# Picking and placing tokens for 32 experts: fp32 one-hot products with transposes become float32r products with two-part operands, on 16 weight slots

## The chip, the cores and the metric

The kernel runs on one core of a Trainium2 chip. The metric is device time in microseconds of one execution, as the median of several runs. Engines are named as in the profile: PE is TensorE's matmul stream, PEld its weight loads, DVE is VectorE, ACT is ScalarE, POOL is GpSimd, SP is SyncE, whose queue issues the loads of the weights.

## The reference, cut to what matters

Two layers of a hybrid block, then a layer with attention and a linear recurrence, and then the part that the change is in, a mixture of 32 experts over 256 tokens of 1024 features. Everything is float32.

```python
def moe_ffn(xn, w_router, b_router, w_gate, b_gate, w_up, b_up, w_down, b_down):
    logits = (xf @ w_router + b_router).astype(jnp.float32)      # xf: 256 x 1024
    top_v, top_i = lax.top_k(logits, TOP_K)                      # 4 of 32 experts
    gates = jax.nn.softmax(top_v, axis=-1).astype(xn.dtype)
    ...                                        # tokens sorted by expert
    def expert_block(args):
        xb, e = args
        g = xb @ w_gate[e] + b_gate[e]         # 1024 x 1024 each
        u = xb @ w_up[e] + b_up[e]
        g = jnp.minimum(g, SWIGLU_LIMIT)
        u = jnp.clip(u, -SWIGLU_LIMIT, SWIGLU_LIMIT)
        glu = g * jax.nn.sigmoid(SWIGLU_ALPHA * g)
        return ((u + 1.0) * glu) @ w_down[e] + b_down[e]
    ...                                        # times the gate, summed into the tokens
```

The layer adds the result to x, and a last rms norm follows.

## The kernel before, in words

Up to about 480 us the first three layers run. Their weights come through the same slots as the experts'. A slot is a tile of 128 x 2048 floats (1 MB) in SBUF; there are 24, and `give` (L235) hands free ones to the list `order` of all weight tiles, in order: for every tile of the list it issues one DMA on the SP queue (L243). `release` (L247) gives a slot back when its tile has been used. For the experts, slots 0 to 3, 8, 9, 13, 15 to 18 and 21 are given first (L1016, L1017), then 4 to 7 and 11 (L1033), then 10 and 14 (L1298): 19 in all. An expert has 12 tiles, four each of gate, up and down.

`router` (L1095) computes the logits, the four gates and, for each token and expert, `rank`, the token's place among that expert's tokens (1000 or more for tokens of other experts), and `count`. It also makes `xh`, the normed x (L1114).

The loop over the experts handles 64 tokens (CAP) of each:

- `pick` (L1178) compares rank with the numbers 0 to 63 (`hot`, 128 tokens x 64 places, for both halves of the tokens), multiplies `hot` transposed with `xh` in fp32 (L1186, PSUM bank xg), copies (L1187), transposes four blocks (L1192) and multiplies them with the norm's gain into `xT` (L1194). `pick` of the next expert is written behind the gating of this one.
- `up` (L1227) multiplies xT with the gate's and the up part's tiles (`product`, L1214, banks g and u; the two halves of 512 columns go to two 64-column halves of the array), with the bias as one float32r product of a one-hot `own` (L1230, L1234).
- `gated` (L1240) is five passes: clamp of g (L1242), tanh on ACT (L1243), a product (L1244), clamp of u (L1245), and the product that gives h (L1246).
- `place` (L1198), at odd experts for two of them: one-hots times gates (`hotw`, L1205), four transposes (L1210, bank st), a copy into `back` (L1212).
- `add`, through `add_pair`, at even experts for the two before: per half of the tokens two fp32 products of `back` with the experts' outputs `ys` (L1266, two buffers of bank cb) and two adds into x on DVE (L1269), each 512 columns.
- The branch `If` at L1278 (`more_up`) runs the same again for an expert with more than 64 tokens. Then gate's and up's eight slots are released. `down` (L1248) transposes h (L1251), copies (L1253) and multiplies with the down tiles (bank y); two copies, one on ACT (L1326) and one on DVE (L1328), give `ys`. The branch at L1284 (`more_down`) handles further tokens, and the four slots of down are released.

The order on each engine is set by a scheduler that takes the instructions by their place in the program as they become ready; an `If` with its body is one unit to it, and instructions outside may be moved past it. So a pick or an add may stand ahead of the branch at L1278 or behind it. In this run two experts have more than 64 tokens: their second passes stand in the trace at about 545 to 590 us and 1440 to 1480 us.

Of the kernel before, what the change touches and what calls it, by code (L numbers as in the profile page):

```python
# [17 lines left out]
CAP = 64  # L18
# [8 lines left out]
def _col_layout():  # L27
    at, off = {}, 0
    for name, n in (
        ("norm0", 8), ("norm1", 8), ("y0", 4), ("y1", 4), ("cw0", 16), ("cw1", 16), ("cb0", 4), ("cb1", 4),  # L30
        ("n1g", 8), ("final", 8), ("cw2", 16), ("cb2", 4), ("ba", 8), ("bi", 8), ("lam", 8), ("og", 8), ("n2g", 8),
    ):
        at[name] = (off, n)
        off += n
    return at, off
# [62 lines left out]
def _prep(i):  # L98
# [52 lines left out]
    put("n2g", a["norm2_g_2"][0])  # L151
    z["cols"] = c
# [43 lines left out]
def _build(tc, T, out):  # L196
# [577 lines left out]
    def mixer(xt):  # L774
# [258 lines left out]
        give(4, 5, 6, 7, 11)  # L1033
# [41 lines left out]
    t22, t23 = slot(22), slot(23)  # L1075
    xh = slot(12).rearrange("p (a b) -> p a b", a=2)
    bias = ew.tile([128, 1024], F32R, name="bias")
    xg, th = t22[:, 0:512], t22[:, 512:1024]
    more_h = [t22[:, 1024:1536], t22[:, 1536:2048], ew.tile([128, 512], F32, name="more")]
    ys, xTs = ([t23[:, o + 512 * k:o + 512 * k + 512] for k in range(2)] for o in (0, 1024))  # L1080
    nc.scalar.dma_start(rbc[0:96, :], T["b_down"])
    gates, rank = (sm(n, 2, 32, bufs=1) for n in ("gates", "rank"))
    count = small.tile([1, 32], I32, name="count", bufs=1)

    t14 = slot(14)

    def split_bias():

        b = t14[:, 256:1280]
        nc.scalar.dma_start(b, T["bias"])  # L1090
        S.activation(bias, b, AF.Copy)
        for p in (slice(32, 64), slice(96, 128)):
            V.tensor_tensor(bias[p], b[p], bias[p].bitcast(F32), op=OP.subtract)

    def router():  # L1095
# [7 lines left out]
        r, _ = x_stats(1e-5, xh, False, True)  # L1103
        tt = [bank(n) for n in ("xg", "tr", "st", "y")]
# [8 lines left out]
        for hf in range(2):  # L1113
            V.tensor_scalar(xh[:, hf, :], x[:, hf, :], r[:, hf:hf + 1], None, op0=OP.mult)  # L1114
# [33 lines left out]
    def last_bias():  # L1148

        t = bank("tr")  # L1150
        gx = ew.tile([128, 2, 192], F32, name="hotw")[:, :, 0:96]
# [15 lines left out]
    four = lambda v: v.rearrange("p (c s t) -> p c s t", c=4, s=2)  # L1167
    gain = cols[:, COLS["n2g"][0]:COLS["n2g"][0] + 8].rearrange("p (s c) -> p c s", s=2)

    def ranks(e, j):  # L1170
        if not j:
            return rank[:, :, e]
        r = sm("rj", 2)
        V.tensor_scalar(r, rank[:, :, e], -64.0 * j, None, op0=OP.add)
        return r

    def pick(e, j):

        r = ranks(e, j)
        one_hot = ew.tile([128, 2, 64], F32, name="hot", bufs=2)  # L1180
# [188 lines left out]
```

## Time and profile before

| | us |
|---|---|
| median of 3 runs | 1564.4 |
| lowest and highest | 1557.71, 1566.32 |
| profiled execution, its own time | 1557.0 |
| span in the profile | 1555.1 |
| PE busy | 1406.8 (90%) |
| DVE busy | 580.6 (37%) |
| ACT busy | 306.7 (20%) |
| moved by DMA | 469.31 MB, mean 302 GB/s |

The page cuts the span in 40 slices of 38.9 us. The timeline lists instructions by start, duration, engine, line, operation and tiles, merged where they follow each other; in brackets stands how long the engine was idle before and what ended that. An fp32 product stands as two records in PE's stream, a float32r product as one. A matmul's duration holds its way through the array, so the work that it costs in a row of them is the spacing of their starts. Tiles that lie in slots are all named s.

### The profile page before, as it was taken

The page shows a single profiled execution, that of the slowest core. Times are in us where ns is not written, and L with a number is a line of the kernel's source. Part 1 is how long each engine was busy: PE and PEld are TensorE (multiplying, and loading weights), DVE is VectorE, ACT ScalarE, POOL GpSimd, SP SyncE. Part 2 cuts the span into 40 slices and gives each one's busy share as a digit, 9 for nine tenths or more (in the row PEclk, how much of TensorE's full clock was granted, in tenths as well). Part 3 has the DMA queues.
Part 4 walks back from the last instruction along what each step waited for, and adds up shares of the span by engine and source line. Part 5 has one row for each costly group of instructions (what it writes and reads, how often), then busy time and mean ns, then how long its engine had stood idle before and what let it go on. Part 6 is the DMA issues. An engine that isn't in the chain of part 4 may idle for free. (4 is left out here: it accounts for less than half of the span.)

```text
span 1555.1 us, 17575 instructions
## 1 busy us (share of the span) xinstructions
PE 1406.8 (90%) x6638; PEld 707.5 (45%) x6638; DVE 580.6 (37%) x1238; ACT 306.7 (20%) x551; POOL 170.8 (11%) x100
## 2 busy tenths in 40 slices
PE   7899989999879989999899999998999998999896
PEld 6687877888556333333333333333333333333332
DVE  4856467648786212222122212221222222222123
ACT  4335443454552000000000000000000000000001
POOL 3333333344240000000000000000000000000001
PEclk9899999999889999999999999999999999999998
DMA  8423443444258756999999999999999999999561
GB/s 296 160 91 127 137 163 109 142 148 139 81 196 337 297 210 264 419 417 370 412 401 420 407 416 408 377 419 418 417 418 410 419 419 406 413 420 419 235 252 63
DMA packets 67500, 469.31 MB, mean 302 GB/s; under 512 B 8128, under 2 KB 9440, under 8 KB 11744
## 3 DMA queue, kind: packets, MB, share of 16 engines
q1 hardware_dynamic: 65664, 463.38, 74.4%
q8 instruction: 142, 2.33, 0.6%
q10 hardware_dynamic: 1632, 3.10, 0.6%
q14 instruction: 62, 0.51, 0.1%
HBM read 465.40 MB, written 1.05 MB: 300 GB/s over the span
## 5 line engine op out<-in xcount | busy, mean ns | idle before, releaser
L1223 PE MATMUL g<-s,s 128*64 128x512 f32 x1088 | 289.4, 601 | 25.3 <-PEq L1284 23.4
L1223 PE MATMUL y<-s,hT 128*64 128x512 f32 x1088 | 256.5, 602 | 1.8 <-ACT hT L1253 1.8
L1223 PE MATMUL u<-s,s 128*64 128x512 f32 x1088 | 247.5, 596 | 0.0
L1223 PEld LDWEIGHTS g<-s,s 128*64 128x64 f32 x1088 | 83.3, 136 | 179.1 <-issue 175.2
L1223 PEld LDWEIGHTS y<-s,hT 128*64 128x64 f32 x1088 | 91.5, 139 | 148.4 <-issue 124.7
L355 POOL TENSOR_TENSOR s<-s,s 128x1024 fp32r<-128x1024 f32 (+2 forms) x59 | 135.3, 2296 | 215.6 <-ACT s L352 163.5
L1223 PEld LDWEIGHTS u<-s,s 128*64 128x64 f32 x1088 | 74.6, 137 | 142.7 <-issue 139.3
L1328 DVE COPY s<-y 64x512 f32<-64x512 f32 x32 | 22.0, 689 | 297.4 <-ACTq L1284 280.6
L1343 POOL TENSOR_TENSOR s<-x,s 128x512 f32<-128x512 f32 x4 | 4.9, 1266 | 1081.2 <-DVE x L1269 1081.2
L352 ACT ACTIVATE s<-s 128x1024 fp32r<-128x1024 f32 (+2 forms) x100 | 100.0, 1008 | 115.9 <-PE pja L370 54.5
L369 PE MATMUL pjb<-s,s 128*128 128x512 f32 (+2 forms) x288 | 101.1, 351 | 7.6 <-DVE s L355 7.6
L368 PE MATMUL pjb<-s,s 128*128 128x512 f32 (+2 forms) x288 | 102.0, 354 | 1.1 <-ACT s L399 0.7
L368 PE MATMUL pja<-s,s 128*128 128x512 f32 (+2 forms) x272 | 98.8, 364 | 3.1 <-ACT s L352 2.6
L370 PE MATMUL pjb<-s,s 128*128 128x512 f32 (+2 forms) x288 | 100.3, 348 | 1.2 <-DVE s L355 0.8
L369 PE MATMUL pja<-s,s 128*128 128x512 f32 (+2 forms) x272 | 97.4, 358 | 3.6 <-DVE s L355 3.6
L370 PE MATMUL pja<-s,s 128*128 128x512 f32 (+2 forms) x272 | 96.7, 355 | 0.5 <-DVE s L400 0.5
L1245 DVE TENSOR_SCALAR s<-u 128x512 f32<-128x512 f32 x34 | 23.5, 692 | 178.2 <-PE u L1223 178.2
L355 DVE TENSOR_TENSOR s<-s,s 128x1024 fp32r<-128x1024 f32 (+2 forms) x53 | 69.4, 1312 | 52.7 <-ACT s L352 52.5
L1242 DVE TENSOR_SCALAR gm<-g 128x512 f32<-128x512 f32 x32 | 22.1, 692 | 161.4 <-PE g L1223 161.4
L1186 PE MATMUL xg<-s,hot 128*64 128x512 f32 x272 | 78.4, 599 | 2.5 <-DVE hot L1182 2.5
L1243 ACT ACTIVATE s<-gm 128x512 f32<-128x512 f32 x32 | 20.2, 630 | 303.2 <-DVE gm L1242 303.2
L1269 DVE TENSOR_TENSOR x<-x,cb 128x512 f32<-128x512 f32 x72 | 49.1, 687 | 64.9 <-PE cb L1266 64.8
(357 smaller groups left out, 1509.8 us busy)
## 6 DMA issues: line engine op xcount, KB each, us to landing
s<-in_w_up_dram SPq DMA_DIRECT2D x128, 1024.0 KB, 18.0
s<-in_w_gate_dram SPq DMA_DIRECT2D x128, 1024.0 KB, 18.1
s<-in_w_down_dram SPq DMA_DIRECT2D x128, 1024.0 KB, 12.3
s<-in_w_o_dram SPq DMA_DIRECT2D x12, 1024.0 KB, 4.8
s<-in_w_cqk_dram SPq DMA_DIRECT2D x4, 1024.0 KB, 7.9
s<-in_w_bqk_dram SPq DMA_DIRECT2D x4, 1024.0 KB, 4.9
s<-in_w_bvg_dram SPq DMA_DIRECT2D x4, 1024.0 KB, 5.0
s<-in_w_aq_dram SPq DMA_DIRECT2D x4, 1024.0 KB, 4.8
```

The lines of the kernel that those rows point to most:

```text
L352: S.activation(h, w, AF.Copy)
L355: (V if el == "V" else G).tensor_tensor(lo, w, h.bitcast(F32), op=OP.subtract)
L368: PE.matmul(d, ah, bh, start=start, stop=False, skip_group_check=True)
L369: PE.matmul(d, ah, bl, start=False, stop=False, skip_group_check=True)
L370: PE.matmul(d, al, bh, start=False, stop=stop, skip_group_check=True)
L1186: ins = PE.matmul(t[64 * c:64 * c + 64, :], one_hot[:, hf, :], xh[:, hf, 512 * c:512 * c + 512], start=hf == 0, stop=hf == 1)
L1223: ins = PE.matmul(t[o:o + 64, :], a[:, kt % 4, kt // 4, :], w[i][:, 1024 * k + 512 * c:1024 * k + 512 * c + 512], start=kt == 0, stop=kt == 7)
L1242: V.tensor_scalar(gm, tt[0], 7.0, None, op0=OP.min)
L1243: S.activation(th, gm, AF.Tanh, scale=0.851)
L1245: V.tensor_scalar(th, tt[1], 7.0, -7.0, op0=OP.min, op1=OP.max)
L1269: V.tensor_tensor(d, d, t[c], op=OP.add)
L1328: cp(ys[c][p, :], t[p, :])
```

## The change

- Slots: 11, 10 and 14 are no longer given to weights; 16 stay. The slots 12, 23, 22, 10, 11 and 14 hold the expert stage's own tiles.
- The normed x is kept as two float32r parts, `xp[0]` (rounded, on ACT) and `xp[1]` (the rest, on DVE).
- `pick(b, q)` makes the transposed inputs of four experts (batch b) at once: for two of the eight blocks of features, four float32r products each of an x block (128 x 128, the weights) with the one-hots of four experts (256 columns), and an ACT pass with the gain. It is called once per expert, a quarter of the next batch at a time; ahead of the loop four times for batch 0. The copies and transposes of the old pick are gone.
- `places(e)`, now for every expert: a one-hot of 128 x 128; one float32r product that spreads the expert's row of ranks over 128 partitions, two of two columns that pick the gates of the places; three small DVE passes, the last of which compares the spread ranks with the place numbers and gives `back`.
- `down` ends with two passes that scale y with the gates and split it in two float32r parts `yp` (ACT, then DVE).
- `scatter(hf)`, for every expert and one expert later: per half of the tokens four float32r products of 64 rows (two parts, two halves of 512 columns) and two adds into x.
- In `more_down` the scatters of the first 64 tokens and `places` come ahead of the second `down`; its own scatter is left to the next expert's.

```diff
-        give(4, 5, 6, 7, 11)
+        give(4, 5, 6, 7)
...
+    xp = [slot(i, F32R).rearrange("p (a b) -> p a b", a=2) for i in (12, 23)]
...
         for hf in range(2):
-            V.tensor_scalar(xh[:, hf, :], x[:, hf, :], r[:, hf:hf + 1], None, op0=OP.mult)
+            S.activation(xp[0][:, hf, :], x[:, hf, :], AF.Copy, scale=r[:, hf:hf + 1])
+            V.scalar_tensor_tensor(xp[1][:, hf, :], x[:, hf, :], r[:, hf:hf + 1], xp[0][:, hf, :].bitcast(F32),
+                                   op0=OP.mult, op1=OP.subtract)
...
+    xTs = [slot(i).rearrange("p (k n) -> p k n", k=8) for i in (22, 10)]
+    f11, f14 = slot(11), slot(14, F32R)
+    hid, th, hT, xTm = (f11[:, o:o + 512] for o in range(0, 2048, 512))
+    yp = [f14[:, o:o + 512] for o in (0, 512)]
+    hot = f14[:, 1024:1536].rearrange("p (a e s) -> p a e s", a=2, e=4)
+    back, hotm = f14[:, 1536:1792], f14[:, 1792:2048].rearrange("p (a s) -> p a s", a=2)
...
+    def one_hots(b):
+
+        for hf in range(2):
+            V.tensor_tensor(hot[:, hf], rank[:, hf, 4 * b:4 * b + 4, None].to_broadcast([128, 4, 64]),
+                            slots[:, None, 0:64].to_broadcast([128, 4, 64]), op=OP.is_equal)
...
+    def places(e, j):
+
+        one_hot(e, j)
         t = bank("st")
+        PE.matmul(t[:, 0:256], idr[:, e:e + 1].to_broadcast([32, 128]), rT, start=True, stop=True)
+        for hf in range(2):
+            PE.matmul(t[:, 256:258], hotm[:, hf, :], gp[:, hf, e, :], start=hf == 0, stop=hf == 1)
+        g, gs = sm("gj", 1), sm("gs", 2)
+        V.tensor_copy(gs, t[:, 256:258])
+        V.tensor_tensor(g, gs[:, 0:1], gs[:, 1:2], op=OP.add)
+        V.tensor_scalar(back, t[:, 0:256], -64.0 * j, col("slotp", 0), op0=OP.add, op1=OP.is_equal)
+        return g
+
+    def pick(b, q):
+
+        t = two(bank("pk"))
+        for i in range(2):
+            kt = 2 * q + i
             for hf in range(2):
+                for k in range(2):
+                    PE.matmul(t[:, i, :], xp[k][:, hf, 128 * kt:128 * kt + 128], hot[:, hf].rearrange("p e s -> p (e s)"),
+                              start=hf + k == 0, stop=hf + k == 2)
+        for i in range(2):
+            S.activation(xTs[b % 2][:, 2 * q + i, :], t[:, i, :], AF.Copy, scale=gain[:, 2 * q + i:2 * q + i + 1])
...
+    def pick_more(e, j):
+
+        one_hot(e, j)
+        t = bank("tr").rearrange("p (k n) -> p k n", k=8)
+        for kt in range(8):
+            for hf in range(2):
+                for k in range(2):
+                    PE.matmul(t[:, kt, :], xp[k][:, hf, 128 * kt:128 * kt + 128], hotm[:, hf, 0:64], start=hf + k == 0, stop=hf + k == 2)
+        V.tensor_tensor(xTm, t, gain[:, :, None].to_broadcast([128, 8, 64]), op=OP.mult)
+        return xTm
...
-    def add(lhs, rhs):
-        for hf in range(2):
-            t = [bank("cb", 2) for _ in range(2)]
+        S.activation(yp[0], t, AF.Copy, scale=g)
+        V.scalar_tensor_tensor(yp[1], t, g, yp[0].bitcast(F32), op0=OP.mult, op1=OP.subtract)
+
+    def scatter(hf):
+
+        t = [bank("cb", 2) for _ in range(2)]
+        for k in range(2):
             for c in range(2):
-                PE.matmul(t[c], lhs(c, hf), rhs(c), start=True, stop=True)
-            for c in range(2):
-                d = x[:, hf, 512 * c:512 * c + 512]
-                V.tensor_tensor(d, d, t[c], op=OP.add)
+                p = slice(64 * c, 64 * c + 64)
+                PE.matmul(t[c], back[p, 128 * hf:128 * hf + 128], yp[k][p, :], start=k == 0, stop=k == 1)
+        for c in range(2):
+            d = x[:, hf, 512 * c:512 * c + 512]
+            V.tensor_tensor(d, d, t[c], op=OP.add)
...
-        gated(t, h, h)
-        if e < 31:
-            cur = pick(e + 1, 0)
-        if e % 2:
-            back = place([(e - 1, 0), (e, 0)], "back")
-        elif e:
-            add_pair()
+        gated(t, hid, hid)
+        if e:
+            scatter(0)
+        if b < 7:
+            pick(b + 1, i)
+        if e:
+            scatter(1)
         if e == 6:
             last_bias()
+        g = places(e, 0)
         n = nc.values_load(count[0:1, e:e + 1], min_val=0, max_val=256)
         more_up(e, w, n, 1)
```

## Rows read from the trace of the kernel before

**Rows 1.** The page: the span, and DMA in 40 slices.
```profile
span 1555.1 us, 17575 instructions
...
DMA  8423443444258756999999999999999999999561
GB/s 296 160 91 127 137 163 109 142 148 139 81 196 337 297 210 264 419 417 370 412 401 420 407 416 408 377 419 418 417 418 410 419 419 406 413 420 419 235 252 63
```

**Rows 2.** Windows: stretch, length, busy PE, PEld, DVE, ACT, POOL, PEclk, DMA share, GB/s.
```profile
611.00:984.00 373.00, 345.42 (x1457) 121.37 (x1456) 87.76 (x178) 28.28 (x47) 0.00 (x0) 0.99 0.99 406
984.00:1410.00 426.00, 393.24 (x1685) 140.76 (x1685) 99.85 (x206) 33.82 (x56) 0.00 (x0) 1.00 1.00 413
```

**Rows 3.** Waits of the SP queue, 984 to 1410: us in total, times, longest.
```profile
SPq L243 <- PEq L1278: 179.2, 15, 18.2
```

**Rows 4.** Waits of PE, 984 to 1410.
```profile
PE g L1223 <- PEq L1284: 15.4, 14, 1.9
PE tr L1251 <- DVEq L1278: 14.6, 14, 1.1
```

**Rows 5.** Timeline, an even expert between u and y.
```profile
1160.85 1.89 PE L1186 MATMUL xg<-s,hot 128*64 128x512 f32 x8
1161.06 0.69 DVE L1245 TENSOR_SCALAR s<-u 128x512 f32<-128x512 f32 x1 [5.37 <-PE u L1223]
...
1162.66 1.13 PE L1266 MATMUL cb<-s,back 128*128 128x512 f32 x2
...
1163.63 0.60 PE L1192 MATMUL tr<-cst,s 128*128 128x128 f32 x4
...
1164.06 2.93 PE L1266 MATMUL cb<-s,back 128*128 128x512 f32 x6
...
1167.03 0.69 DVE L1269 TENSOR_TENSOR x<-x,cb 128x512 f32<-128x512 f32 x1 [0.36 <-PE cb L1266]
...
1168.12 0.63 PE L1251 MATMUL tr<-cst,gm 128*128 128x128 f32 x4 [1.13 <-DVEq L1278]
```

**Rows 6.** Timeline of DVE, the odd expert before it.
```profile
1131.35 0.69 DVE L1245 TENSOR_SCALAR s<-u 128x512 f32<-128x512 f32 x1 [5.37 <-PE u L1223]
...
1135.57 0.23 DVE L1230 TENSOR_SCALAR own<-cst 128x128 fp32r<-128x128 f32 x1 [0.40 <-DVEq L1278]
```

**Rows 7.** Groups by line and form, whole span: busy us, mean ns, idle before.
```profile
L355 DVE TENSOR_TENSOR s<-s,s 128x1024 fp32r<-128x1024 f32 x48 | 64.7, 1350 | 35.9 <-ACT s L352 35.8
...
L399 ACT ACTIVATE s<-tr,cols 128x256 fp32r<-128x256 f32 x20 | 9.4, 472 | 19.6 <-PE tr L407 15.8 <-DVE s L400 3.8
```

**Rows 8.** Timeline of PE, an expert of the stretch 611 to 984.
```profile
767.11 0.63 PE L1251 MATMUL tr<-cst,gm 128*128 128x128 f32 x4 [1.88 <-DVEq L1278]
...
771.97 1.45 PE L1186 MATMUL xg<-s,hot 128*64 128x512 f32 x5
...
779.82 1.88 PE L1266 MATMUL cb<-s,back 128*128 128x512 f32 x4
```

**Rows 9.** Timeline of PE, first layer: float32r products of 512 and of 256 columns.
```profile
200.47 0.39 PE L370 MATMUL pjb<-s,s 128*128 128x512 f32 x1
200.70 0.28 PE L368 MATMUL pja<-s,s 128*128 128x256 f32 x1
200.81 0.28 PE L369 MATMUL pja<-s,s 128*128 128x256 f32 x1
```

**Rows 10.** Timeline of PE, attention scores: fp32 products of 64 rows.
```profile
408.72 1.16 PE L898 MATMUL sc<-s 64*128 64x256 f32 x8
```

**Rows 11.** Timeline of PE: the start of u ahead of rows 5.
```profile
1153.39 5.32 PE L1223 MATMUL u<-s,s 128*64 128x512 f32 x24
```

**Rows 12.** Timeline of DVE, the normed x ahead of the router's passes.
```profile
486.23 1.41 DVE L1114 TENSOR_SCALAR s<-x,rr 128x1024 f32<-128x1024 f32 x2
```

**Rows 13.** Timeline of PE, from the first pick to the first g.
```profile
492.10 1.94 PE L1186 MATMUL xg<-s,hot 128*64 128x512 f32 x8
...
496.23 0.64 PE L1223 MATMUL g<-s,s 128*64 128x512 f32 x1
```

More of the change, by code (lines that the diff above doesn't have):

```diff
@@ L1074, in _build @@
     ew = ctx.enter_context(tc.tile_pool(name="ew", bufs=1))
-    t22, t23 = slot(22), slot(23)
-    xh = slot(12).rearrange("p (a b) -> p a b", a=2)
     bias = ew.tile([128, 1024], F32R, name="bias")
-    xg, th = t22[:, 0:512], t22[:, 512:1024]
-    more_h = [t22[:, 1024:1536], t22[:, 1536:2048], ew.tile([128, 512], F32, name="more")]
-    ys, xTs = ([t23[:, o + 512 * k:o + 512 * k + 512] for k in range(2)] for o in (0, 1024))
+    more_h = [ew.tile([128, 512], F32, name=f"more{j}") for j in range(3)]
     nc.scalar.dma_start(rbc[0:96, :], T["b_down"])
@@ L1102, in router @@
         load_row(br, "br")
-        r, _ = x_stats(1e-5, xh, False, True)
-        tt = [bank(n) for n in ("xg", "tr", "st", "y")]
+        r, _ = x_stats(1e-5, two(slot(22)), False, True)
+        tt = [bank(n) for n in ("pk", "tr", "st", "y")]
         x_T(0, [two(t) for t in tt])
@@ L1166, in _build @@
     nc.scalar.dma_start(b_down, T["b_down_end"])
[L1167 to L1180, printed above, removed]
-        for hf in range(2):
-            V.tensor_scalar(one_hot[:, hf, :], slots[:, 0:64], r[:, hf:hf + 1], None, op0=OP.is_equal)
-        t = bank("xg")
-        for hf in range(2):
-            for c in range(2):
-                ins = PE.matmul(t[64 * c:64 * c + 64, :], one_hot[:, hf, :], xh[:, hf, 512 * c:512 * c + 512], start=hf == 0, stop=hf == 1)
-        S.activation(xg, t, AF.Copy)
-        if e + j == 0:
-            busy(ins, 2, bank("cb", 2))
-        t = bank("tr")
-        for c in range(4):
-            PE.transpose(t[:, 128 * c:128 * c + 128], xg[:, 128 * c:128 * c + 128], ident)
-        xT = four(more_h[j - 1] if j else xTs[e % 2])
-        V.tensor_tensor(xT, four(t), gain[:, :, :, None].to_broadcast([128, 4, 2, 64]), op=OP.mult)
-        return xT
@@ L1284, in more_down @@
         with tc.If(n > CAP * j, label=f"down{e}_{j}"):
-            y = more_h[j - 1]
-            t = down(y, w)
-            busy(last[0], 4, bank("cb", 2))
-            S.activation(y, t, AF.Copy)
-            back = place([(e, j)], "backm")
-            half = lambda c: slice(64 * c, 64 * c + 64)
-            add(lambda c, hf: back[half(c), 128 * hf:128 * hf + 128], lambda c: y[half(c), :])
+            if j == 1:
+                scatter(0)
+                scatter(1)
+            g = places(e, j)
+            down(more_h[j - 1], w, g)
             if j < 3:
+                with tc.If(n > CAP * (j + 1)):
+                    scatter(0)
+                    scatter(1)
                 more_down(e, w, n, j + 1)
-    cur = pick(0, 0)
+    one_hots(0)
+    rank_rows()
+    for q in range(4):
+        pick(0, q)
     split_bias()
-    give(10, 14)
-    back = None
-    def add_pair():
-        add(lambda c, hf: back[:, 256 * c + 128 * hf:256 * c + 128 * hf + 128], lambda c: ys[c])
     for e in range(32):
@@ L1331, in _build @@
             release(i0 + k)
-    add_pair()
+    for hf in range(2):
+        scatter(hf)
+    t22, t23 = slot(22), slot(23)
+    xh = two(slot(12))
     fr = t22[:, 0:1024]
```

85 lines of the change are left out of this document (47 added, 38 removed).

## The prediction

> **What bounds the kernel now.** I read the page's slices first [rows 1]: from slice 17 the DMA row stands at 9 and the rate at 370 to 420 GB/s; it falls only in the last three. The windows by stage [rows 2] say the same more sharply: share 0.99 and 1.00, 406 and 413 GB/s. An expert has 12 weight tiles of 128 x 2048 fp32, 12.58 MB, so 413 GB/s is 30.5 us for an expert and 406 is 31.0. The best slices hold 419 to 420 GB/s: at that rate an expert costs 30.0 us. That is the floor, and the loop stands 0.5 to 1.0 us above it.
>
> Which of the two leads, the queue or TensorE? The queue's own waits [rows 3] name TensorE's branch at L1278: 179 us of 426, 15 times, for a slot that is not free yet. TensorE's waits [rows 4] name no weight at all; they name the branch at L1284 (15.4 us) and VectorE before the transposes of h (14.6 us). So TensorE, with VectorE behind it, still leads, and the queue follows with almost nothing to spare. A faster expert gains only down to 30.0 us: 373 us x (1 - 406/419.5) + 426 us x (1 - 413/419.5) = 12.0 + 6.6 = 18.6 us is all that lies between 611 and 1410, and some 8 us more if the queue may fall behind by the slack worked out under the slots.
>
> The Trainium skill's page "DMA: Bandwidth & Descriptors" (Where 436 GB/s comes from) says that for loads from HBM the HBM side, about 358 GB/s a core, binds. By that an expert could not come below 35.1 us and no edit of TensorE's work would show; this trace disagrees with 413 GB/s over 426 us, so that rule gets no chance of its own.
>
> **The change part by part.** The products of gate, up and down, the biases and the gating stay. What moves is the work between u and y, and it stands at two places.
>
> Late branch (984 to 1410, 14 experts). The branch L1278 waits until VectorE has done everything ahead of it. In the even expert shown [rows 5] that is clamp at 1161.06, h, one multiply of the transposed tokens, four adds (the last 1167.03 to 1167.72), branch over at 1168.12: 7.06 us. In the odd one [rows 6], without adds, 1131.35 to 1135.57: 4.22 us. Mean 5.64. After the change every expert is alike: clamp and h 1.46 (two of 0.69 and the step between), four adds at 0.69, 2.76, a gap before the second pair because scatter(1) needs the cb banks that the first pair frees (0.5; between 0 and 1.0, as three products of 0.23 and a latency fit beside it), back 0.48 (a pass of 256 columns out of PSUM, as the ACT one of L399, 0.47 [rows 7]), and 0.40 to get going again as in [rows 6]. That is 5.6 with back ahead of the branch and 5.1 with it behind. I take 5.4: 0.25 us x 14 = **3.5 us** gained. Bounds: 5.1 (gain 7.6 us) and 7.06, every expert as the even one now (loss 20 us).
>
> Early branch (611 to 984, 12 experts). Here the branch follows h at once, the pick runs inside y and the adds inside g [rows 8]: VectorE is off the path and TensorE's own work counts. Removed per expert: pick 1160.85 to 1162.66, 1.81, four transposes 0.60 and half of eight half-products at 0.43 (the spacing of 1164.06's group: 2.93 us for six), 1.72, in all 4.1 [rows 5]. Added: pick, eight float32r products of 256 columns at 0.11 to 0.12, 0.96 [rows 9]; scatter, eight of 512 columns at 0.23, 1.84, or half if the two 64-row halves run side by side, as eight 64-row fp32 records of 256 columns in 1.16 us suggest [rows 10]; places, three at most 0.12, 0.36. In all 2.2 to 3.2. Then the changes between 128-row, 64-row, 32-row and 64-column products. One such insertion is in the trace: u with its bias takes 1153.39 [rows 11] to 1160.85 [rows 5], 7.46, where 16 pairs at 0.43 are 6.88 and the inserted product 0.23, so two changes cost 0.35, or 0.18 each. Some four more in an expert: 0.7. Removed minus added is 0.2 to 1.2; I take 0.7 x 12 = **8.4 us**.
>
> A rule that speaks against the change: the Trainium skill's "TensorEngine Tiling (Array Packing)" (Key Properties) says that a change of tiling mode drains TensorE. The trace agrees, with the 0.35 us just shown. Without it the early stretch would gain 0.9 to 1.9 an expert and run into the floor; with it the gain stays below.
>
> Other experts (0 to 3 and 29 to 31, paced by TensorE): 0.3 us x 7, **2 us**. The two overflow passes: pick_more's 32 products of 64 columns at about 0.12 are 3.8 us against the 4 us of a pick; the second pass's four adds and its places now stand ahead of its down instead of behind it. 0, between -2 and +2.
>
> yp takes the place of ys behind y: one ACT and one DVE pass in a row then as now, 0. If that pair were longer, only the adds of the next expert would wait, a whole product later.
>
> Start. The input's two parts are two ACT passes and then two DVE passes of some 1.35 (the row of L355, [rows 7]) where 1.41 us for both is now [rows 12], ahead of the router's DVE chain: +1.4. The first four picks go through one PSUM bank: 0.96 for products and 0.9 for two ACT passes (the row of L399) each, about 8 us, against 492.10 to 496.23 now [rows 13]; g may start on the first quarter. Together some +4 (0 to +6), less 1 at expert 0's branch, which has no adds: **+3**.
>
> Slots 19 to 16. Nothing in the steady loop depends on the count: 8 tiles are issued at one branch and 4 at the other, now as then. What shrinks is the lead. The four up tiles of the next expert are now issued at the branch, with 10 us of queue time (4 x 2.5, a tile of 1.05 MB at 419 GB/s), and u begins 17.8 us behind it (1135.57 to 1153.39, [rows 6, 11]): some 8 us to spare. Ahead of the loop and at both overflows the queue stands still 3 x 2.5 = 7.5 us earlier; that lies beside TensorE's work, as slices 14 to 16 at 297, 210 and 264 GB/s show an idle queue there [rows 1]. 0; without that cover 3 x 7.5 = 22 us.
>
> Sum: -3.5 - 8.4 - 2 + 3 = -10.9. The profiled execution took 1557.0 us (span 1555.1 [rows 1] and 1.9 around it): 1546.1. The median of the runs is 7.4 above it: 1553.5, said as **1553**.
>
> **The rivals.**
> B, the floor is reached. If the branch stands early everywhere, 26 experts gain 0.7 to 1.2, 18 to 31 us, and the queue at 419 GB/s cuts that at 18.6 and a part of its slack. For it: that order stands in this kernel [rows 8]. Against: half of the loop has the other [rows 5, 6]. Some 24 us: 1540.
> C, a wait takes the place of the removed work. back is one tile, and may not be rewritten before scatter(1) has read it, so the chain is 5.6, as 5.64 now; the mode changes eat the early stretch, and the start costs 3: 1563.
> D, slower. The odd experts' short section vanishes: every expert has four adds on VectorE, and if they wait for cb as the even ones do now, each takes 7.06 in place of 5.64: 1.42 x 28 = 40 us and 3 at the start, 1607; with half of it, 6.35, 1587. It decides from a mean chain of about 5.8 us, (7.8 - 3)/28 above today's, if the early stretch gives nothing. For it: the last adds of an even expert wait for cb [rows 5]. Against: the products that fill cb shrink from 0.43 x 2 to 0.23.
> That float32r does not deliver is small: this form of product stands at 0.11 and 0.23 in the trace [rows 9].
>
> **How the numbers follow.** A measurement of this kernel tells about 0.5%, 7.8 us, from no change. My forecast A has 0.45, with its own range 1543 to 1561; 0.36 of it lies below 1556.6, 0.09 above. B has 0.14, all faster. C has 0.18, no change. D has 0.23, slower. So faster 0.50, same 0.27, slower 0.23. The range leaves out a little of B and the upper half of D: 1532 to 1586.
>
> **What would show it.** Right: xg and its transposes gone; pk products at 0.12; the stretch of saturated DMA at 415 GB/s or more; clamp to next own near 5.4 in odd and even experts alike; TensorE's waits beginning to name weights. Wrong: a chain from clamp to own above 5.8 in every expert, with DMA below 413 (D); scatter products at more than 0.23; a first g behind 500; TensorE waiting for up tiles with a queue that stands still before (then the slots count after all).

## The result and the profile after

The changed kernel takes 1574.75 us in the median of 20 runs (1566.95 to 1587.98); the kernel before, run beside it on the same chips, 1562.78 (20 runs, 1556.95 to 1576.0). The ratio is 1.0083, with a 95% interval of 1.0056 to 1.0111: slower, where faster was forecast. The profiled execution took 1569.53 us against 1557.01, its span is 12.6 us longer than before's.

The page after, its span, TensorE's busy row, the granted clock in 40 slices, and DMA (the last two answer to [rows 1]):

```profile
span 1567.7 us, 17837 instructions
...
PE 1409.3 (90%) x6694; PEld 712.3 (45%) x6694; DVE 599.2 (38%) x1282; ACT 319.0 (20%) x584; POOL 170.8 (11%) x100
...
PEclk9899999999889989999999999999999999999898
DMA  7423342434156746999899999999999999999562
GB/s 291 161 88 128 136 165 105 153 134 156 63 205 244 303 184 277 381 416 413 367 417 417 396 418 418 416 397 417 416 396 418 416 392 417 418 409 418 241 273 94
```

The windows, with the columns of [rows 2] (PEclk is third from the end):

```profile
611.00:984.00 373.00, 340.61 (x1489) 119.22 (x1489) 93.92 (x192) 33.02 (x60) 0.00 (x0) 0.98 0.98 400
984.00:1410.00 426.00, 387.67 (x1661) 132.18 (x1659) 105.30 (x214) 36.85 (x66) 0.00 (x0) 0.97 1.00 410
1410.00:1505.00 95.00, 85.17 (x357) 31.63 (x353) 21.99 (x48) 5.11 (x8) 0.00 (x0) 0.91 0.78 319
```

TensorE's clock was 0.99 and 1.00 of full speed in the two middle stretches before; now it is 0.98 and 0.97, and 0.91 around the second overflow, where it was 1.00. The queue moves 400 and 410 GB/s in place of 406 and 413. TensorE's largest waits after (the answer to [rows 4]), here over the whole span:

```profile
PE tr L1281 <- DVEq L1309: 49.1, 32, 1.9
PE y L1252 <- ACT s L1282: 20.3, 27, 0.8
```

The same two over the whole span before, the wait for VectorE ahead of the transposes of h and the wait for ScalarE's copy ahead of y:

```profile
PE tr L1251 <- DVEq L1278: 41.0, 30, 1.9
...
PE y L1223 <- ACT hT L1253: 1.8, 3, 0.7
```

The first has grown by 8 us, the second is all but new. The queue's largest waits after (the answer to [rows 3]), over the whole span too:

```profile
SPq L244 <- PEq L1309: 418.2, 31, 36.2
...
SPq L244 <- PEq L1317: 143.2, 27, 21.3
```

No wait for a weight tile stands among TensorE's. What is new is the shape of the gap between u and y. One expert in the middle, on VectorE and TensorE:

```profile
1049.90 0.69 DVE L1274 TENSOR_SCALAR s<-u 128x512 f32<-128x512 f32 x1 [5.37 <-PE u L1252]
...
1050.63 0.69 DVE L1275 SCALAR_TENSOR_TENSOR s<-s 128x512 f32<-128x512 f32 x1
...
1051.74 0.63 PE L1281 MATMUL tr<-cst,s 128*128 128x128 f32 x4 [1.88 <-DVEq L1309]
1051.75 0.23 DVE L1259 TENSOR_SCALAR own<-cst 128x128 fp32r<-128x128 f32 x1 [0.43 <-DVEq L1309]
...
1053.12 8.78 PE L1252 MATMUL y<-s,s 128*64 128x512 f32 x32 [0.75 <-ACT s L1282]
```

VectorE is through fast: from the clamp (1049.90) to own (1051.75) are 1.85 us, and adds and places stand elsewhere. But TensorE does nothing from 1049.86 to 1051.74, works 0.63 us, waits 0.75, and then needs 8.78 us for y. Before, the pick's work broke up that place. In the later experts its products and transposes stood ahead of the transposes of h [rows 5]. In the earlier ones the 1.88 us ahead of the transposes were idle too [rows 8], but two products of the pick stood behind them, while ScalarE copies:

```profile
767.67 1.07 PE L1186 MATMUL xg<-s,hot 128*64 128x512 f32 x2
768.49 3.68 PE L1223 MATMUL y<-s,hT 128*64 128x512 f32 x16
```

The granted clock of the stretch after:

```profile
1050.00:1053.30 3.30, 0.81 (x6) 0.60 (x8) 1.51 (x3) 0.60 (x1) 0.00 (x0) 1.00 1.02 420
1053.30:1056.70 3.40, 3.40 (x10) 0.99 (x10) 0.00 (x0) 0.00 (x0) 0.00 (x0) 0.52 1.00 412
1056.70:1060.00 3.30, 3.30 (x16) 1.01 (x14) 0.00 (x0) 0.00 (x0) 0.00 (x0) 0.97 1.02 412
```

Behind the two waits the clock falls to the lower of its two levels (1.2 GHz, half of 2.4), and y's first part runs at half speed. The same 736 records of y between 700 and 1400 us, by line (count, busy us, mean ns, idle ahead of them), before:

```profile
L1223 PE MATMUL y<-s,hT 128*64 128x512 f32 x736 | 174.6, 602 | 0.0
```

and after:

```profile
L1252 PE MATMUL y<-s,s 128*64 128x512 f32 x736 | 185.7, 661 | 14.4 <-ACT s L1282 14.3
```

Where are the picks, which could fill the gap? A timeline of the picks in the expert before that one:

```profile
1010.39 1.10 PE L1228 MATMUL pk<-s,s 128*128 128x256 f32 x7 [0.57 <-ACT s L1231]
...
1013.29 0.38 PE L1228 MATMUL pk<-s,s 128*128 128x256 f32 x1
1014.60 0.62 PE L1228 MATMUL pk<-s,s 128*128 128x256 f32 x3 [0.93 <-ACT s L1231]
...
1017.35 0.75 PE L1228 MATMUL pk<-s,s 128*128 128x256 f32 x5
...
1019.89 1.21 PE L1228 MATMUL pk<-s,s 128*128 128x256 f32 x8
1022.48 0.63 PE L1281 MATMUL tr<-cst,s 128*128 128x128 f32 x4 [1.37 <-DVEq L1309]
1022.86 0.96 PE L1228 MATMUL pk<-s,s 128*128 128x256 f32 x6
```

With two more at 1027.44 these are all 32 products of a batch, in one expert: half of them inside u, a quarter in the gap behind it, and the rest behind the transposes. The next ones come at 1133.87. The source calls a quarter for each expert; the scheduler pulls the four quarters together (the one-hots for them are ready at once). So of four experts one carries all the picks, and three have empty gaps.

**Where the 12.6 us are.** The start of the last of u's 32 products in each pass cuts the expert stage in stretches that compare across versions. The passes are counted from 0; the two overflow passes are number 2 and 31, so pass 4 is expert 3 and pass 29 expert 28 (the expectations below call these idx, or "expert 4 to 29"; their 25.6 and 29.6 us for the first expert are the second column here, with an end ten products earlier). "Half" is the time that the trace's clock records show at half rate between 485 and 1530 us. All in us, of the profiled executions.

| version | router's first product to u's last of pass 0 | 0 to 4 | 4 to 29 (per pass) | 29 to 33 | half |
|---|---|---|---|---|---|
| before | 28.1 | 125.3 | 764.9 (30.60) | 125.4 | 10.2 |
| after | 32.1 | 129.5 | 767.4 (30.70) | 127.1 | 71.7 |

The router's first product begins 1.5 us later (483.4 to 484.9) and what follows the last u is 1.2 us shorter: 1.5 + 4.0 + 4.2 + 2.5 + 1.7 - 1.2 = 12.7. The middle (passes 4 to 29), from which the forecast took most of its gain, is 2.5 us longer. Each stretch is that of one profiled execution. What stands ahead of the router ended between 481.1 and 496.4 us in the profiles of all the versions here, with 41.0 to 81.9 us at half rate in it, though no edit was aimed at it; the 1.5 us are well inside that.

If a stretch at half rate costs half its length, the 61.5 us more of it are 30.7 us, and by this estimate the changed kernel at before's clock would be 30.7 - 12.6 = 18 us faster than before. That was the first theory, **T1**: the emptied gap, and those around the overflow, let the clock fall, and that takes more than the change gives. The rivals: **T2**, 16 slots are too few; **T3**, the new products and adds are longer themselves. A fourth, **F**, came up behind the first runs: the weight queue sets the pace.

### The profile page after: what moved, and what is told of

It reads as the page before. It is cut to its first block, busy times and chain, and to the rows that moved or that the text cites. A ratio compares the mean times of both kernels' runs of the same rounds, so it can differ in the third digit from the quotient of the medians.

```text
span 1567.7 us, 17837 instructions
## 1 busy us (share of the span) xinstructions
PE 1409.3 (90%) x6694; PEld 712.3 (45%) x6694; DVE 599.2 (38%) x1282; ACT 319.0 (20%) x584; POOL 170.8 (11%) x100
## 5 line engine op out<-in xcount | busy, mean ns | idle before, releaser
L1252 PE MATMUL g<-s,s 128*64 128x512 f32 x1088 | 298.4, 613 | 7.9 <-PEq L1317 4.3
L1252 PE MATMUL y<-s,s 128*64 128x512 f32 x1088 | 266.6, 645 | 20.5 <-ACT s L1282 20.3
L1252 PEld LDWEIGHTS y<-s,s 128*64 128x64 f32 x1088 | 81.5, 147 | 180.3 <-issue 150.7
L1289 DVE SCALAR_TENSOR_TENSOR s<-y,gj,s 128x512 fp32r<-128x512 f32 x34 | 25.5, 751 | 331.7 <-ACTq L1317 315.7
L1252 PEld LDWEIGHTS g<-s,s 128*64 128x64 f32 x1088 | 77.5, 138 | 156.2 <-issue 153.0
L1300 DVE TENSOR_TENSOR x<-x,cb 128x512 f32<-128x512 f32 x136 | 87.6, 684 | 85.8 <-PE cb L1297 85.5
L1272 ACT ACTIVATE s<-s 128x512 f32<-128x512 f32 x32 | 20.2, 631 | 335.8 <-DVE s L1271 335.8
L1288 ACT ACTIVATE s<-y,gj 128x512 fp32r<-128x512 f32 x34 | 23.4, 687 | 274.0 <-PE y L1252 242.3
L1282 ACT ACTIVATE s<-tr 128x512 f32<-128x512 f32 x34 | 20.3, 597 | 228.5 <-PE tr L1281 228.5
```

Of the source, the lines that this page charges most:

```text
L1252: ins = PE.matmul(t[o:o + 64, :], a(kt), w[i][:, 1024 * k + 512 * c:1024 * k + 512 * c + 512], start=kt == 0, stop=kt == 7)
L1272: S.activation(th, gm, AF.Tanh, scale=0.851)
L1282: S.activation(hT, t.rearrange("p (c s t) -> p c s t", c=4, s=2), AF.Copy, scale=0.5)
L1288: S.activation(yp[0], t, AF.Copy, scale=g)
L1289: V.scalar_tensor_tensor(yp[1], t, g, yp[0].bitcast(F32), op0=OP.mult, op1=OP.subtract)
L1300: V.tensor_tensor(d, d, t[c], op=OP.add)
```

## The experiments

Ratios are to the kernel before on the same chip. Diffs are against the changed kernel where nothing else is said.

### Idle products in the gap, four and eight

```diff
-        if e == 31:
-            busy(last[0], 4, bank("pk"))
+        busy(last[0], 4, bank("pk"))
```

> After, with four idle fp32 products on TensorE behind the u product of every expert (so far behind the last one alone), in the stretch of about 1.9 us in which TensorE waits for h to be made. Nothing of the result changes. T1 (the granted clock: TensorE falls to half for 3.4 us at a time behind the emptied gap, and that costs more than the change saves): the windows at half between 640 and 1440 us fall from 14 to 4 or fewer, the mean of one y product from 656 ns (700 to 1560 us) towards 602, the middle 765 us shorten by 10 to 25 us (DMA at about 410 GB/s then stands close behind), and the run takes 1545 to 1560 us against the 1569.5 us of after's profiled run: 0.985 to 0.998 of before. T2 (16 slots starve the weights): no change, within 3 us of after. T3 (the new products and adds are themselves longer): the fills only add work, 0 to +1 us for an expert, up to 30 us slower.

The second run has 8 in place of 4:

> As the run with four idle products, with eight: a dose. T1: the windows at half stay as few as with four, or fewer; the time is within 5 us of that with four, unless the eight products are longer than the gap, which then costs up to 1 us for each of 28 experts. T2 and T3: no gain over after; T3 up to 40 us slower.

Measured: 1575.13 us, 1.0084 (1.0050 to 1.0118), and 1576.74 us, 1.0101 (1.0069 to 1.0134). No gain. T1's half came true: time at half rate falls from 71.7 to 44.4 and 41.0 us, in the middle from 44.4 to 17.1 and 10.2. But passes 4 to 29 take 769.7 and 774.1 us. The timeline of the version with four shows why:

```profile
986.80 1.16 PE L1058 MATMUL pk<-one 128*128 128x128 f32 x8
988.02 1.60 PE L1228 MATMUL pk<-s,s 128*128 128x256 f32 x8
989.45 0.60 PE L1281 MATMUL tr<-cst,s 128*128 128x128 f32 x4
991.03 7.09 PE L1252 MATMUL y<-s,s 128*64 128x512 f32 x32 [0.98 <-ACT s L1282]
```

y is at 7.09 us, full speed, and the scheduler spreads the picks now: eight stand behind the fill. Fill and picks together are 2.65 us (986.80 to 989.45) where the gap was 1.88; what the clock gave back, the longer gap seems to have taken. These runs changed two things at once, fill and place of the picks, and settle neither.

### Before with 16 slots

```diff
-        give(4, 5, 6, 7, 11)
+        give(4, 5, 6, 7)
...
-    give(10, 14)
```

(against the kernel before)

> Before, with its three later weight slots not given, so that 16 serve throughout, and nothing else changed. T1: the slots carry nothing of the difference, 0.997 to 1.003 of before. T2 (slots): slower by 0.8% (12 us) or more, with waits of TensorE for weights (DMA) in the middle. T3: no change.

Measured: 1570.23 us, 1.0046 (1.0012 to 1.0081): between the two expectations. In the trace TensorE never waits for a weight tile. But the edit moved more than the slots: in 19 experts of the built program picks and adds stand at other places in TensorE's order (an overflow's next expert has them inside g instead of behind u). So this run doesn't tell slots from order; the one with 14 slots below does, for the kernel after. Its order does show something else: all 25 passes of the middle now have 1.67 to 1.88 us idle ahead of the transposes, with the pick's products behind them, and the clock fell in 2 of the 25.

### The picks in the gaps

```diff
         gated(t, hid, hid)
...
+        if b < 7:
+            with tc.issue_after(last[0].ins):
+                pick(b + 1, i)
...
-        if b < 7:
-            pick(b + 1, i)
```

(the new lines stand ahead of `gated`)

> After, with the eight pick products of each quarter issued behind the u product of their own expert, so that they stand in that expert's gap between u and the transposes of h, where after bunches all 32 in every fourth expert's. No work is added. T1: the gap is filled in all experts of seven of the eight stages, windows at half fall from 14 to 4 or fewer, y's mean falls towards 602 ns; the middle shortens by 10 to 25 us, 1545 to 1560 us in all. T2: no change. T3: within 5 us of after, as the work is the same.

Measured: 1569.48 us, 1.0053 (1.0018 to 1.0088). 44.4 us at half in all, 3.4 in the middle; passes 4 to 29 take 758.9 us (30.36 each), 8.5 less than after's. T1 was right on the clock, a little too hopeful on the middle, and 9.5 us too hopeful on the whole, whose interval still overlaps after's: passes 29 to 33 take 131.5 us, 4.4 more than after's. In the middle something new ends the waits, with [rows 2]'s rates reached or passed:

```profile
PE u L1252 <- DMA s<-in_w_up_dram: 11.0, 24, 1.1
PE g L1252 <- DMA s<-in_w_gate_dram: 7.5, 13, 0.7
```

```profile
611.00:984.00 373.00, 346.97 (x1553) 122.62 (x1551) 100.04 (x204) 35.11 (x64) 0.00 (x0) 1.00 0.99 408
984.00:1410.00 426.00, 382.60 (x1671) 127.30 (x1667) 104.36 (x213) 37.12 (x67) 0.00 (x0) 1.00 1.01 413
```

For the first time TensorE waits for weights, 37 times for gate's and up's tiles. At 413 GB/s the 12.58 MB of an expert take 30.5 us, about what a pass takes: here the queue sets the pace, and before's 30.60 us a pass stand within 0.3 of it.

### Eleven weight tiles in place of twelve

To see TensorE's own pace, one tile in twelve is left out: the last quarter of the down product takes the third quarter's tile again, so these outputs are not the reference's.

```diff
-        order += [(n, (e, h), 512) for n in ("w_gate_2", "w_up_2", "w_down_2") for h in range(4)]
+        order += [(n, (e, h), 512) for n in ("w_gate_2", "w_up_2", "w_down_2") for h in range(4)][:11]
...
-        i0 = nsec + 12 * e
-        w = [loaded[i0 + k][0] for k in range(12)]
+        i0 = nsec + 11 * e
+        w = [loaded[i0 + min(k, 10)][0] for k in range(12)]
```

Before, after, and the version with the picks in the gaps:

> Before with eleven weight tiles for an expert in place of twelve: the last quarter of the down product takes the third quarter's tile again, so that the fourth is neither loaded nor used (another output). Every product on TensorE stays. A new theory F stands beside T1 now: in the middle (expert 4 to 29, 25 periods of 30.6 us in before, 30.7 in after, 30.35 with the picks in the gaps) the weight queue sets the pace at 406 to 414 GB/s in every version, so that saved TensorE work cannot show there, and what makes after slower lies outside: the first expert (25.6 to 29.6 us), the two overflow passes, the three slots. F: with 11/12 of the bytes the queue would need 28.1 us; before's period falls to TensorE's own pace, 29 to 30 us, 15 to 40 us in all. T1, and my forecast, by which TensorE leads and the queue only follows: before changes by less than 8 us.

> After with the same eleven tiles. F: the half-clock windows stay, so the period is TensorE's, (3 x 28.5 + 34.0) / 4 = 29.85 us at full clock and 0.4 to 0.9 more with one window in most experts: 30.2 to 30.7, hardly under today's 30.7; after gains 0 to 12 us and before_w11 is faster than it by 15 us or more. T1 alone: after gains nothing, and the distance to before_w11 stays as it is between after and before, 12 us.

> The version with every expert's picks in its own gap, with the same eleven tiles: this is the new TensorE work at full clock without the queue's bound. F: period 28.5 to 29 us against 30.35 with twelve tiles, 35 to 45 us less in all, and faster than before_w11: the change's saving on TensorE is there and the queue hides it. If the new work saves nothing: no faster than before_w11.

Measured: 1554.7 us, 0.9899 (0.9841 to 0.9957); 1574.36 us, 1.0076 (1.0040 to 1.0112); 1533.7 us, 0.9803 (0.9754 to 0.9852).

After does not move: with a twelfth fewer bytes it takes what it took (1.0083). So its pace is TensorE's, and the queue has nothing to do with its loss; passes 4 to 29 take 770.5 us, and 75.1 us in all are at half. Before gains 1.0% by its ratio, some 16 us (7 to 25 by its interval, from four runs), and 8.8 us by the medians: the low end of F's 15 to 40 us by the one, hardly more than the forecast's view allowed by the other. It is 19.7 us ahead of after with eleven tiles, as F wanted (15 or more). As the order of its picks moved in this build too, how much of its gain is the queue's stays open. The third is the answer on the change itself: with the gaps filled and the queue out of the way a pass takes 29.12 us (728.1 in the middle), and the run is 1.0% faster than before with eleven tiles (by the two intervals 0.2 to 1.7%, from four runs each). So with its picks in the gaps the new work on TensorE is the shorter one, if not by much beyond the noise.

```profile
611.00:984.00 373.00, 348.53 (x1563) 123.53 (x1559) 100.28 (x207) 35.18 (x64) 0.00 (x0) 1.00 0.95 387
984.00:1410.00 426.00, 395.55 (x1776) 141.34 (x1774) 110.31 (x230) 38.36 (x69) 0.00 (x0) 1.00 0.98 398
```

### The clock by itself

Two more with eleven tiles, in which TensorE's order is all but that of the last one, apart from the picks and the fill. First the eight picks of a quarter move from the gap to the place behind y:

```diff
-        if b < 7:
-            with tc.issue_after(last[0].ins):
-                pick(b + 1, i)
...
         down(hid, w, g, f"down{e}_1")
+        if b < 7:
+            with tc.issue_after(last[0].ins):
+                pick(b + 1, i)
```

> The version with the picks in the gaps and eleven weight tiles, with the eight picks of each quarter moved from the gap behind u to the place behind y: evenly spread, but the gap stays empty in every expert. Nothing else moves, and no work is added. (One weight tile in twelve is left out, as before: the queue is out of the way.) If only the bunching of the picks cost after its time: 1.2 us more for each of 28 experts, a period of 29.7 us, 33 us slower than with the picks in the gaps (1534 us). T1 (the clock): on top of that a half-clock window behind most gaps, 1.7 us each, a period of 30.3 to 31.4, 50 to 75 us slower, 1584 to 1609 us, and 15 or more windows between 640 and 1440.

Then five idle products go into the gap of every expert (`busy(last[0], 5, bank("pk"))` behind u):

> The same, picks behind y and eleven tiles, with five idle fp32 products in the gap behind u of every expert, some 1.4 us of the 1.9 us that it lasts, so that they lengthen nothing. T1: the half-clock windows go (4 or fewer between 640 and 1440), the period comes down to 29.5 to 29.9 and the run is 15 to 40 us faster than without the fill, although TensorE does more. If the clock is not it: the same as without the fill, or slower.

Measured: 1581.54 us, 1.0126 (1.0073 to 1.0178), without the fill; 1562.54 us, 0.9991 (0.9960 to 1.0023), with it. **More work on TensorE, and 19.0 us less time.** The gap in the first:

```profile
1025.59 0.63 PE L1281 MATMUL tr<-cst,s 128*128 128x128 f32 x4 [1.87 <-DVEq L1309]
1026.97 8.56 PE L1252 MATMUL y<-s,s 128*64 128x512 f32 x32 [0.75 <-ACT s L1282]
```

and in the second:

```profile
1048.60 1.38 PE L1058 MATMUL pk<-one 128*128 128x128 f32 x10
1050.54 0.63 PE L1281 MATMUL tr<-cst,s 128*128 128x128 f32 x4 [0.56 <-DVEq L1309]
1051.91 7.09 PE L1252 MATMUL y<-s,s 128*64 128x512 f32 x32 [0.75 <-ACT s L1282]
1058.93 1.21 PE L1228 MATMUL pk<-s,s 128*128 128x256 f32 x8
```

The 32 records of y take 8.56 us in the one and 7.09 in the other. The same 0.75 us wait for ACT is left in both; with 0.56 us idle ahead of the transposes in place of 1.87 the clock holds. Time at half: 68.3 and 20.5 us. In the middle alone it goes from 23.9 to none; half of that is 12.0 us, and the passes 4 to 29 are 11.7 us shorter (771.1 to 759.4). The expectation for the first had 15 or more falls between 640 and 1440 us, and there were 8, so it came out 2.5 us below its fast end; the second's passes take 30.38 us, not 29.5 to 29.9: with the picks in the gap they take 29.12, more than was reckoned with, and eight picks on the path add 1.26.

The y of the version with the fill, by line, 700 to 1400 us, the same 736 records as in after:

```profile
L1252 PE MATMUL y<-s,s 128*64 128x512 f32 x736 | 163.0, 595 | 16.6 <-ACT s L1282 16.5
```

163.0 us, where after has 185.7: 22.7 less, and half of the 44.4 us that after spends at half rate in the middle is 22.2. The Trainium skill's page "TensorE: Matmul & The Clock Gate" (HAM oscillation — how this bites in real kernels) describes a loop in which a wait ahead of every tile throttles the clock again each time, and puts the cost at half of the time spent throttled. On the cost the runs agree, with these two numbers; here, though, the clock did not fall each time (behind 13 of the 19 passes of after's middle that have both waits). There the wait is for DMA, here for VectorE and ScalarE.

The other part is the picks' place: from 1562.5 to 1533.7, 28.8 us, for moving them into a gap that is there anyway.

### Idle products in the overflow passes

Twelve tiles again, the picks in the gaps, and fills in the waits of the overflow passes and behind u in the last four experts (which have no picks):

```diff
     def pick_more(e, j):
+        busy(None, 12, bank("g"))
         one_hot(e, j)
...
+        busy(None, 6, bank("g"))
         V.tensor_tensor(xTm, t, gain[:, :, None].to_broadcast([128, 8, 64]), op=OP.mult)
...
             gated(up(e, lambda kt: xT[:, kt, :], w), more_h[j - 1], more_h[j - 1])
+            busy(last[0], 10, bank("y"))
...
-        if e == 31:
-            busy(last[0], 4, bank("pk"))
+        if b == 7:
+            busy(last[0], 8, bank("pk"))
```

(and four ahead of the overflow's y)

> The version with the picks in the gaps, and idle fp32 products in the waits of the overflow passes (12 ahead of the overflow's picks, 6 behind them, 10 behind its u, 4 ahead of its y) and behind u in the last four experts, which have no picks. T1: the 20 to 24 us at half clock between 548 and 590 and between 1440 and 1490 shrink to 7 or fewer, the two overflow passes (idx 2 to 3 and 31 to 32 of u: 42.4 and 44.0 us in after, 38.7 and 38.8 in before) fall to 39 to 41, and the run gains 4 to 9 us over the version with the picks in the gaps alone: 0.998 to 1.002 of before. F says the same of these stretches, as the queue idles there. Rival: the fills only push the gaps, no gain.

Measured: 1570.13 us, 1.0054 (1.0017 to 1.0091): the rival was right on the time. Only 3.4 us at half are left around each overflow, as T1 said, but passes 29 to 33 still take 130.1 us; the fills seem to be longer than the gaps and to push them. With some half of them, for the first overflow of an expert alone (6, 3, 5, none ahead of y, 5 behind u):

> Twelve tiles, the reference's output. The picks in the gaps, and fills of the overflow that are no longer than its gaps: half of those of the run before last (6, 3 and 5 in place of 12, 6 and 10, none ahead of the overflow's y, the first overflow of an expert alone, so that less code stands in the branches), and 5 in place of 8 behind u in the last four experts. T1: the four experts around each overflow (u's ends 30 to 34: 95.7 us in before, 101.3 in after, 103.1 to 103.5 with and without the long fills) take 95 to 98 us at full clock, the whole 1555 to 1566 us in the median, 0.995 to 1.002 of before. Rival: the passes are longer by their products and by a first expert of 29.6 us in place of 25.6 whatever the clock does, 1.004 to 1.008.

Measured: 1558.04 us, 0.9973 (0.9937 to 1.0009), 16.7 us less than after and no longer slower than before. Passes 29 to 33 take 122.8 us, 2.6 less than before's, 0 to 4 take 121.4, 3.9 less. The overflow's picks in after, whose 32 products start at 1444.94:

```profile
1440.99 1.94 PE L1252 MATMUL u<-s,s 128*64 128x512 f32 x8
1444.94 6.04 PE L1240 MATMUL tr<-s,s 128*128 128x64 f32 x32 [2.01 <-DVE s L1206]
1451.77 7.57 PE L1252 MATMUL g<-s,s 128*64 128x512 f32 x24 [0.78 <-DVE s L1241]
```

and with the fills:

```profile
1436.86 1.38 PE L1058 MATMUL pk<-one 128*128 128x128 f32 x10
1438.07 1.50 PE L1058 MATMUL g<-one 128*128 128x128 f32 x12
1439.33 3.75 PE L1242 MATMUL tr<-s,s 128*128 128x64 f32 x32
1442.91 1.62 PE L1058 MATMUL g<-one 128*128 128x128 f32 x6
```

3.75 in place of 6.04 us for the same 32 products.

These two versions speak against reading the clock off the length of a wait alone. Their order in the middle is that of the version with the picks in the gaps, but they have 37.5 and 34.1 us at half there in place of 3.4, and passes 4 to 29 take 763.6 us each time in place of 758.9. Every fourth expert waits 1.37 us ahead of the transposes and 0.75 ahead of y, in all three: behind this the clock fell 5, 4 and 1 times in 6. The other falls stand behind waits of 2.2 to 5.3 us at the branch behind y.

A last version adds 15 in place of 8 idle products behind the router, and 3 ahead of the picks in every gap:

> The last version (picks in the gaps, short fills in the overflows and in the last four experts) with two more fills: 15 in place of 8 idle products behind the router's second half, where TensorE waits 1.95 us longer for the ranks than the old fill lasts, and 3 ahead of the picks in every expert's gap, some 0.8 of the 1.4 us still idle there. T1: no 10 us window at half in the first expert (two of the profiles so far, and the last version's, show one at 494 us, which makes that expert 34.0 us instead of 29.6), hardly any in the middle; 0 to 5 us gained on average, 0.993 to 0.998 of before. Rival: the middle is the queue's anyway and the fills lengthen experts whose gap is shorter: 0.997 to 1.004.

Measured: 1560.94 us, 0.9982 (0.9950 to 1.0015). Half falls to 27.3 us, the start is without the long fall of the version before (32.1 us in place of 36.5; after has 32.1 without that fill), and the time is the same within the intervals, as the rival had it: the middle stands at the queue's rates again (408 and 413 GB/s, 30.36 us a pass), and there are 27.5 us of waiting at the branch behind y.

### Fewer slots

```diff
-        give(4, 5, 6, 7)
+        give(4, 5)
```

> After with two more weight slots taken away, 14 in place of 16; the order of the instructions on TensorE stays all but the same here (44 lines of some 8,000 differ), where taking three slots from before had moved products in 19 experts too. If the slots carry a part of the loss (before with 16 gave 1.0046): 1.012 to 1.02 of before, and TensorE begins to wait for weight tiles. If TensorE sets the pace and the lead is ample: 1.006 to 1.011, as after, and no wait for weights.

Measured: 1577.62 us, 1.0099 (1.0059 to 1.0140), against after's 1.0083 (1.0056 to 1.0111). Passes 4 to 29 take 767.4 us, as in after, and one wait of 0.2 us for a weight tile stands in the trace. Two slots fewer cost nothing that shows.

| version | us | ratio | to u's last of pass 0 | 0 to 4 | 4 to 29 (per pass) | 29 to 33 | half |
|---|---|---|---|---|---|---|---|
| 4 / 8 idle products in the gap | 1575.1 / 1576.7 | 1.0084 / 1.0101 | 32.1 / 36.5 | 127.8 / 126.2 | 769.7 (30.79) / 774.1 (30.96) | 127.3 / 126.5 | 44.4 / 41.0 |
| picks in the gaps | 1569.5 | 1.0053 | 33.6 | 125.2 | 758.9 (30.36) | 131.5 | 44.4 |
| with short fills | 1558.0 | 0.9973 | 36.5 | 121.4 | 763.6 (30.55) | 122.8 | 51.2 |
| 14 slots | 1577.6 | 1.0099 | 32.1 | 129.9 | 767.4 (30.70) | 129.5 | 75.1 |
| after, 11 tiles | 1574.4 | 1.0076 | 32.1 | 126.8 | 770.5 (30.82) | 127.1 | 75.1 |
| picks in the gaps, 11 tiles | 1533.7 | 0.9803 | 32.1 | 123.7 | 728.1 (29.12) | 123.6 | 34.3 |
| picks behind y, 11 tiles | 1581.5 | 1.0126 | 36.5 | 129.8 | 771.1 (30.84) | 125.1 | 68.3 |
| the same with a fill | 1562.5 | 0.9991 | 33.6 | 127.5 | 759.4 (30.38) | 122.0 | 20.5 |

## Why the prediction was wrong

The forecast was 1553 us, faster; measured are 1574.75, inside the range of 1532 to 1586 but on its slow side.

**The step that failed** is the early branch (-8.4 us), and with it the late one (-3.5). Both took off work and left the rest at the speed of before; TensorE's clock stood in no term. The prediction called VectorE "off the path" in the early experts, though the first row of [rows 8] has TensorE waiting 1.88 us for it; behind that wait the clock fell in 2 of 11 passes before. It read in [rows 5] and [rows 8] that the pick stands around the transposes of h, counted it as work removed, and did not name what stands there afterwards: nothing, a second wait right behind the first, and then in 13 of 25 passes a clock at half rate. In the middle of after 44.4 us are at half; 767.4 - 22.2 = 745.2 us would by this estimate be the same work at full clock, 19.7 less than before's 764.9 (16.3 less, if before's own 6.8 us at half are taken off too). Split at pass 15, where before's order changes, the 16.3 are 5.7 early, where 8.4 was forecast, and 10.5 late, where 3.5 was: there the branch's chain came to some 2 us, not 5.4. So the saving was there, more than the 11.9 forecast, and the clock took it back; how much of it the queue would have let through stands under rival B. That emptied gaps are enough for this was shown, with eleven tiles, by the run whose five idle products made it 19 us faster.

**Where the pick stands** was taken for granted too: "the pick runs inside y". All 32 products of a batch stand in one expert of four. With eleven tiles, spread behind y and into the gap they differ by 28.8 us, and the bunched ones of after stand 40.7 us behind those in the gap (1574.4 and 1533.7).

**The cost of the new work** came out in its range. Eight picks take 1.14 us by spacing (498.78 to the next product at 499.92 in after), against 0.96; the scatter's four products 0.67 (in the version with four fills 1000.95 to 1001.62), so 1.34 for eight where 1.84, or half, was said; places' three 0.62, where 0.36 was said. In all 3.1, in the range of 2.2 to 3.2, at its dear end. The changes between forms were reckoned too dear: u's 24 records of [rows 11] stand 0.219 us apart (the bias product comes at 1158.64), so 16 pairs are 7.00 us, not 6.88, and two changes cost 0.23, not 0.35. What they cost among the new products no run takes apart.

**Rival D** did not happen, though it had the right sign. From clamp to own are 1.85 us, and 1.63 to 2.48 in all of the middle, not 7.06 nor the 5.4 of the forecast: the adds and back no longer stand ahead of the branch. The early experts of before had 1.63 to 1.84 already. **Rival C** named a wait in the place of the removed work, but the one for back ahead of the adds, at today's speed, and no change as the outcome; the waits that came stand around the transposes.

**Rival B**, the floor, is real and lies higher than 30.0 us: with the picks in the gaps TensorE waits for weights at 408 and 413 GB/s and 30.36 us a pass. The best slices' 420 GB/s are not held over an expert. Had the clock stayed up, the middle could have gained some 6 us (764.9 to 758.9), not 18.6.

**The start** (+3, between 0 and 6) measured +5.5: 1.5 ahead of the router, which the spread of that part covers, and 3.9 between the first g (497.78, not behind 500, [rows 13]) and the end of the first u, where three quarters of the picks stand between g's products. **The overflows** (0, between -2 and +2) measured +4.2 and +1.7 in their stretches, with 10.2 and 17.1 us at half there; in the version with picks in the gaps and short fills they are gains. **The slots** (0) were right as far as it was tried: 14 cost what 16 cost, and TensorE waited for no weight tile in after.

Open is what the kernel before would gain from less weight traffic, as its order could not be kept, why before with 16 slots lost 0.5%, for the same reason, and why the clock falls behind the same two waits in one pass and not in another.

## What to carry to other kernels

Ask of every product that a change takes away what TensorE does in its place: where the answer is "it waits for another engine", price the clock, and look at the mean of the next big product as the first sign. Move work that is needed anyway into that gap, and if there is none, idle products no longer than the gap; the longer ones gained nothing here. And look up in the built order where the scheduler puts a piece that can go anywhere: here its place was worth more than its cost.

## What the runs showed of the hardware that was not expected

Two short waits close together, once in an expert of 30 us, were enough for the granted clock to fall to 1.2 GHz, in a kernel whose TensorE is 90% busy. In the middle of after 19 of 25 passes have 1.67 to 1.88 us idle, 0.6 us of transposes and another 0.75 us idle; the clock fell behind 13 of these and behind none of the other six. One of the two alone hardly did it. With the first and the pick's products in place of the second it fell behind 2 of 11 (before) and 2 of 25 (before with 16 slots); with the second and 0.36 to 0.56 us ahead of the transposes, behind none (picks behind y, with the fill).

The lengths do not settle it: with the picks behind y and no fill all 25 passes have both waits at full length, and it fell behind 7. What decides between these passes no run here shows.

In the overflow the fall lasted longer (10.2 us at 1446 in after), with 32 products of 64 columns in it, which are short; they then take 0.19 us each in place of 0.12.
